# Three chained transformer layers on one core: the squares of queries and keys as a stream of their own, the last weights of an output product in the keys' buffers, a zero-padded compressed-value product

## The chip, the cores and the metric

One core of one Trainium2 chip runs the whole program. The core has five engines with an instruction queue each: PE (the 128x128 matrix array), DVE (elementwise work and reductions), ACT (activation functions and copies), POOL (general work) and SP (which here issues DMA transfers). Each engine runs its own queue in order, and an instruction waits there until its semaphores are reached. The metric is the device time of one execution in microseconds (us), median of several runs.

## The reference

512 tokens of width 1024 pass three layers. Only what the change touches is written out:

```
layer 1   q, kc_raw, vc_raw, ks, vs, kw, vw, gates, hq, hf, hi, hg = split(rms_norm(x) @ w_in)
          q  = rms_norm(q per head of 64)             # 8 heads; needs the sum of squares of each row of a head
          ks, kw = rms_norm(...)                      # 2 key groups each, the same sums
          kc, vc = rms_norm(compress(kc_raw)), compress(vc_raw)      # 31 compressed keys and values
          o_nsa  = g0 * softmax(q kc) vc + g1 * softmax(q ks) vs + g2 * softmax(q kw) vw
          o_hgrn = gated linear recurrence over chunks of 64 (4 heads)
          x = x + concat(o_nsa, o_hgrn) @ w_out       # 1024 x 1024
          x = x + (silu(gate) * up) @ w_down          # gated feed-forward, width 2816
layers 2, 3   stick-breaking attention (8 heads of 64) and differential attention (4 heads),
          x = x + concat(sb, df) @ w_o                # 1024 x 1024
          x = x + relu(h @ w_ff1)^2 @ w_ff2           # width 4096
```

All is float32.

## The kernel before

The residual stream X lies in SBUF as eight tiles [128 features x 512 tokens]. A product by a weight matrix streams the weights in blocks of 512 KB through `load_w` (L376): SP issues the DMA into one of three raw buffers, ACT casts it to a rounded copy `hi` (L395), DVE writes the remainder `lo` (L396), both into rings of two buffers. Each product tile is then three matmuls, `mm3` (L401 to L403): hi by high half, lo by high half, hi by low half. `gemm_fm` (L411) walks the blocks of a matrix and hands each finished bank of PSUM to an `emit` function; a block of an output product covers four groups k of 128 input rows and two tiles of 128 output features.

The program is written by Python generators that a planner interleaves. `Clock` (L74) keeps an estimate of when each engine is free and when each tile is written and last used; `_drive` (L171) asks the streams in a fixed order for their next step, and a stream whose tiles aren't ready by the estimate (`ready`, `bank_free`) is passed over. In layer 1 the streams are the linear recurrence (`hgrn_all`), the preparation of the sparse attention (`nsa_setup`), its attention proper (`nsa_attention`), and last the dense products (`dense1`), which fill what the others leave. A scheduler then orders each engine's instructions by that priority and their dependencies; weight loads have their priority raised by a lookahead.

What the change touches:

- `emit_nsa` (L776) gets the projections of queries (m = 0 to 3) and keys (m = 4, 5), 64 features of two heads each. It evacuates them (`nq`, `nraw`), has ACT square them (`nsq`, L789), and at once issues four PE matmuls by a block matrix of ones (`pq`, L792; each is two instructions in the trace) and the copy of the sums to `qss` (L795, L798). The dense stream's next matmuls stand behind these on PE. `nsa_setup` goes on from `qss` to the norms.
- `gemm_late` (L464) is the half of the output product whose operand, the last mixer outputs, comes late: for its blocks 0 and 1 it does row groups 0 to 2, then waits for row group 3 (`hs[3]`), finishes the four tiles, and passes blocks 2 and 3 to `gemm_fm`, named `wout0x` in layer 1, `L0wo1x` and `L1wo1x` in layers 2 and 3. It starts when the attention's last scores are issued (`"scored"`): block 0 then takes two spare banks that the scores used (`wl0`, `wl1`; in layers 2 and 3 a pair, `L0wl`), block 1 the two `mm` banks. The weights of block 2 and 3 wait for a free pair of the hi and lo ring.
- `values` (L1021) of the sparse attention runs once for each unit (4 head pairs i, 4 query blocks, 2 branches). In branch 0 it first opens the bank `po` with the compressed values: `comp["v"]` holds four copies of 32 rows, and the product contracts 32 rows of it, placed at row 32 i of the array (L1028).
- In layers 2 and 3 the differential attention runs units of one query block: `scores2`, `turn2` (transposes, `dpt`), `values2` (`dfo`, L1337), and `head_squares` (L529), where ACT squares the output of the unit out of the same bank `dfo` that the next unit's matmuls write to. After a head's last unit its norm is taken, the output is transposed (`do_t`, L558) and split into `do_m_h` (ACT, L561) and `do_m_l` (DVE, L562), which are `hs` of `gemm_late`.

## Time and profile before

| | us |
|---|---|
| time, median of 3 runs | 2017.0 (2017.0 to 2017.1) |
| profiled execution: its own time | 2017.01 |
| its span in the trace | 2015.1 |
| PE busy | 1974.8 (98%) |
| DVE busy | 1176.9 (58%) |
| ACT busy | 885.1 (44%) |
| POOL busy | 45.2 (2%) |
| mean granted clock of TensorE | 0.993 |

PE is busy for all but some 40 us of the span. The profile gives the granted TensorE clock by stretches: 1.00 stands for 2.4 GHz and 0.50 for 1.2 GHz. PE's waits are listed by the instruction that waited and the one that released it; a window gives the busy time of each engine in a stretch of the span.

### The profile page before, as it was taken

The page shows a single profiled execution, that of the slowest core. Times are in us where ns is not written, and L with a number is a line of the kernel's source. Part 1 is how long each engine was busy: PE and PEld are TensorE (multiplying, and loading weights), DVE is VectorE, ACT ScalarE, POOL GpSimd, SP SyncE. Part 2 cuts the span into 40 slices and gives each one's busy share as a digit, 9 for nine tenths or more (in the row PEclk, how much of TensorE's full clock was granted, in tenths as well). Part 3 has the DMA queues.
Part 4 walks back from the last instruction along what each step waited for, and adds up shares of the span by engine and source line. Part 5 has one row for each costly group of instructions (what it writes and reads, how often), then busy time and mean ns, then how long its engine had stood idle before and what let it go on. Part 6 is the DMA issues. An engine that isn't in the chain of part 4 may idle for free.

```text
span 2015.1 us, 25957 instructions
## 1 busy us (share of the span) xinstructions
PE 1974.8 (98%) x10197; PEld 1610.1 (80%) x10197; DVE 1176.9 (58%) x2032; ACT 885.1 (44%) x1497; POOL 45.2 (2%) x87
## 2 busy tenths in 40 slices
PE   8999999999999999999999999999999999999998
PEld 7888866788888878787778888888888778888887
DVE  7687676744444456557764444447466874444446
ACT  6645355522222235687542223335587743322223
POOL 1000000000000000001000000000000000000000
PEclk9999899999999999999999999999999999999999
DMA  6212100122222222212122222223221222222222
GB/s 206 67 60 88 51 22 22 53 95 96 99 97 95 95 89 92 82 40 84 61 84 98 100 95 94 94 94 105 79 64 58 63 76 98 98 94 94 95 94 74
DMA packets 50922, 168.65 MB, mean 84 GB/s; under 512 B 5808, under 2 KB 8240, under 8 KB 50800
## 3 DMA queue, kind: packets, MB, share of 16 engines
q1 hardware_dynamic: 47680, 161.93, 23.4%
q0 software_dynamic: 2976, 4.98, 1.2%
q8 instruction: 81, 1.33, 0.3%
q14 instruction: 41, 0.34, 0.1%
q10 hardware_dynamic: 144, 0.07, 0.0%
HBM read 160.14 MB, written 2.10 MB: 81 GB/s over the span
## 4 chain that ended last, share of the span: by engine, by line
PE 88%; DVE 5%; ACT 5%; issue 2%; DMA 1%; SPq 0%; DVEq 0%; POOL 0%; ACTq 0%
PE L0wf_p L403 6%; PE L0wf_p L401 6%; PE L0wf_p L402 6%; PE L1wf_p L403 5%; PE L1wf_p L401 5%; PE L1wf_p L402 5%; PE wgu_p L403 4%; PE wgu_p L401 4%; PE wgu_p L402 4%; PE wdn_p L401 2%; PE wdn_p L402 2%; PE wdn_p L403 2%; PE po L1033 1%; PE hpl L695 1%; PE pt L1014 1%
## 5 line engine op out<-in xcount | busy, mean ns | idle before, releaser
L395 ACT CAST L0wf_h<-L0wf_r 128x1024 fp32r<-128x1024 f32 x64 | 67.3, 1051 | 228.1 <-PE L0wf_p L403 224.8
L395 ACT CAST L1wf_h<-L1wf_r 128x1024 fp32r<-128x1024 f32 x60 | 63.1, 1051 | 219.7 <-PE L1wf_p L403 216.7
L403 PE MATMUL wgu_p<-h_l,wgu_h 128*128 128x512 f32 x328 | 128.8, 393 | 0.0
L401 PE MATMUL wgu_p<-h_h,wgu_h 128*128 128x512 f32 x328 | 128.7, 392 | 0.0
L402 PE MATMUL wgu_p<-h_h,wgu_l 128*128 128x512 f32 x328 | 128.6, 392 | 0.0
L395 ACT CAST wgu_h<-wgu_r 128x1024 fp32r<-128x1024 f32 x44 | 46.2, 1050 | 162.9 <-issue 62.8
L401 PE MATMUL L0wf_p<-L0u_h,L0wf_h 128*128 128x512 f32 x256 | 100.7, 393 | 0.0
L402 PE MATMUL L0wf_p<-L0u_h,L0wf_l 128*128 128x512 f32 x256 | 100.4, 392 | 0.0
L403 PE MATMUL L0wf_p<-L0u_l,L0wf_h 128*128 128x512 f32 x256 | 99.4, 393 | 0.0
L403 PE MATMUL L0wf_p<-L0m_l,L0wf_h 128*128 128x512 f32 x240 | 94.2, 393 | 0.0
L403 PE MATMUL L1wf_p<-L1m_l,L1wf_h 128*128 128x512 f32 x240 | 94.2, 393 | 0.0
L401 PE MATMUL L0wf_p<-L0m_h,L0wf_h 128*128 128x512 f32 x240 | 94.2, 392 | 0.0
L401 PE MATMUL L1wf_p<-L1m_h,L1wf_h 128*128 128x512 f32 x240 | 94.2, 392 | 0.0
L402 PE MATMUL L1wf_p<-L1m_h,L1wf_l 128*128 128x512 f32 x240 | 94.1, 392 | 0.0
L402 PE MATMUL L0wf_p<-L0m_h,L0wf_l 128*128 128x512 f32 x240 | 94.1, 392 | 0.0
L396 DVE TENSOR_TENSOR L0wf_l<-L0wf_r,L0wf_h 128x1024 fp32r<-128x1024 f32 x64 | 78.4, 1226 | 24.7 <-ACT L0wf_h L395 24.7
L401 PE MATMUL L1wf_p<-L1u_h,L1wf_h 128*128 128x512 f32 x224 | 88.1, 393 | 0.0
L402 PE MATMUL L1wf_p<-L1u_h,L1wf_l 128*128 128x512 f32 x224 | 87.9, 392 | 0.0
L396 DVE TENSOR_TENSOR L1wf_l<-L1wf_r,L1wf_h 128x1024 fp32r<-128x1024 f32 x60 | 73.5, 1225 | 23.2 <-ACT L1wf_h L395 23.2
L403 PE MATMUL L1wf_p<-L1u_l,L1wf_h 128*128 128x512 f32 x224 | 86.9, 393 | 0.0
L491 DVE TENSOR_TENSOR X<-X,L0wf_p 128x512 f32<-128x512 f32 x64 | 44.0, 687 | 67.1 <-PE L0wf_p L403 67.1
L491 DVE TENSOR_TENSOR X<-X,L1wf_p 128x512 f32<-128x512 f32 x56 | 38.6, 689 | 66.5 <-PE L1wf_p L403 66.5
(879 smaller groups left out, 5397.2 us busy)
## 6 DMA issues: line engine op xcount, KB each, us to landing
L0wf_r<-w_ff SPq DMA_DIRECT2D x64, 512.0 KB, 3.2
L1wf_r<-w_ff SPq DMA_DIRECT2D x60, 512.0 KB, 3.3
wgu_r<-w_gu SPq DMA_DIRECT2D x44, 512.0 KB, 3.2
wdn_r<-w_dn SPq DMA_DIRECT2D x22, 512.0 KB, 3.2
wns_r<-w_nsa SPq DMA_DIRECT2D x8, 512.0 KB, 3.5
L0wsb_r<-w_sbqk SPq DMA_DIRECT2D x8, 512.0 KB, 3.2
L0wdf_r<-w_dfqk SPq DMA_DIRECT2D x8, 512.0 KB, 3.2
L1wsb_r<-w_sbqk SPq DMA_DIRECT2D x8, 512.0 KB, 3.2
```

Of the source, the lines that this page charges most:

```text
L395: S.copy(hi[:, c], raw[:, c])
L396: V.tensor_tensor(lo[:, c], raw[:, c], _f(hi)[:, c], ALU.subtract)
L401: TE.matmul(ps, lh, rh, start=start, stop=False)
L402: TE.matmul(ps, ll, rh, start=False, stop=False)
L403: TE.matmul(ps, lh, rl, start=False, stop=stop)
L491: V.tensor_tensor(X[m], X[m], ps, ALU.add)
L695: TE.matmul(pl[:, b * 64 : (b + 1) * 64], ke[:, b * P : (b + 1) * P], qr[:, b * 64 : (b + 1) * 64], start=True, stop=True)
L1014: TE.transpose(pt[:, o + j * P : o + (j + 1) * P], p[g][:, j * P : (j + 1) * P], ident)
L1033: TE.matmul(po[g * 64 : (g + 1) * 64, 0:P], vsw[:, j, br * 128 + g * 64 : br * 128 + (g + 1) * 64], p[g][:, j * P : (j + 1) * P], start=Fa ...
```

## The change

Four parts.

1. The sums of squares. `emit_nsa` only squares and puts the tile in a list `waiting`. A new stream `nsa_squares`, the first that the planner asks, issues the `pq` matmuls and the copy to `qss` when the square is ready by the estimate and a bank of kind `t` is free; the next `emit_hgrn`, `emit_gate` or `emit_nsa` issues what still waits (`catch_up`).
2. `gemm_late` loads blocks 0 and 1 without waiting for the last scores. Block 0 takes the `mm` banks, block 1 waits for `scored` and takes the spare banks, and at that point the weights of block 2 are loaded into buffers of the keys (`kh`, `kl`), so that `gemm_fm` finds them there.
3. The compressed values lie in `vz`, 128 rows by four blocks of 128 columns, zero but for 32 rows each, written by POOL (a memset and four copies); the product contracts all 128 rows.
4. In layers 2 and 3 the planner holds `values2` of a head's later units until the last reader of the head's bank is done by the estimate (`Clock.read`).

```diff
@@ Clock
+    def read(self, tile):
+        self.take()
+        e, at = self.used.get(tile.tensor.name, ("PE", 0.0))
+        while e != "PE" and self.free["PE"] < at + 0.2:
+            yield None
@@ gemm_fm
-            wh, wl = load_w(src[b], f"{name}_{b}")
+            wh, wl = loaded.pop(0) if loaded else load_w(src[b], f"{name}_{b}")
@@ gemm_late
-    def gemm_late(src, hs, emit, name, banks):
-        tiles, banks = [], list(banks)
+    def gemm_late(src, hs, emit, name, scored, spare_banks):
+        tiles = []
         cols = src.shape[3]
         yield from until(lambda: all(x is not None for x in hs[:3]))
+        loaded = [load_w(src[b], f"{name}_{b}") for b in range(2)]
         for b in range(2):
-            wh, wl = load_w(src[b], f"{name}_{b}")
+            wh, wl = loaded[b]
+            if b == 1:
+                yield from until(scored)
+                loaded = [load_w(src[2], f"{name}_2", ("kh", "kl"))]
+                banks = spare_banks()
             for m in range(cols // P):
-                ps = banks.pop(0)() if banks else bank("mm", f"{name}_p{b}_{m}")
+                ps = bank("mm", f"{name}_p{b}_{m}") if b == 0 else banks[m]
...
-        yield from gemm_fm(src[2:], hs, emit, name + "x", 2 * (cols // P))
+        yield from gemm_fm(src[2:], hs, emit, name + "x", 2 * (cols // P), loaded=loaded)
@@ block1
+        def add_squares():
+            m, sq = waiting.pop(0)
+            pq = bank("t", f"pq{m}")
+            for tb in range(NB):
+                TE.matmul(pq[:, 2 * tb : 2 * tb + 2], sq[:, tb * P : (tb + 1) * P], blk2, start=True, stop=True)
...
+        def catch_up():
+            while waiting:
+                add_squares()
+        def nsa_squares():
+            while len(squared) < 6:
+                yield from until(lambda: waiting or len(squared) == 6)
+                if not waiting:
+                    return
+                m, sq = waiting[0]
+                for w in (ready(sq), bank_free("t", 2)):
+                    for _ in w:
+                        if not waiting or waiting[0][0] != m:
+                            break
+                        yield None
+                if waiting and waiting[0][0] == m:
+                    add_squares()
+                    yield "low"
         def emit_nsa(m, ps):
+            catch_up()
...
             S.activation(sq, ps, AF.Square)
-            pq = bank("t", f"pq{m}")
...
+            waiting.append((m, sq))
@@ nsa_setup
-            yield from until(lambda: 1 in kraw, lambda: nq[3] is not None)
+            yield from until(lambda: len(squared) == 6)
@@ nsa_attention
-                        TE.matmul(po[g * 64 : (g + 1) * 64, 0:P], comp["v"][32 * i : 32 * i + 32, g * 64 : (g + 1) * 64],
-                                  pct[g][32 * i : 32 * i + 32, qs], start=True, stop=False, tile_position=(32 * i, g * 64))
+                        TE.matmul(po[g * 64 : (g + 1) * 64, 0:P], vz[:, i * P + g * 64 : i * P + (g + 1) * 64],
+                                  pct[g][:, qs], start=True, stop=False)
...
+            vz = sb("hs", "vz")
+            G.memset(vz, 0.0)
+            for i in range(4):
+                r = slice(32 * i, 32 * i + 32)
+                G.tensor_copy(vz[r, i * P : (i + 1) * P], comp["v"][r])
@@ dense1
-            yield from until(lambda: "scored" in comp)
...
-        _drive(clock, hgrn_all(), nsa_setup(), nsa_attention(), dense1())
+        _drive(clock, nsa_squares(), hgrn_all(), nsa_setup(), nsa_attention(), dense1())
@@ layer
-                     lambda n: both(ready(st[n], dv[NB - 1]), bank_free("o", 1) if n % NB == 0 else ()))))
+                     lambda n: both(ready(st[n], dv[NB - 1]), bank_free("o", 1) if n % NB == 0 else clock.read(st["do"])))))
```

In the instruction orders below a row is a line of the program, an operation, the tile it writes and those it reads; the line numbers of the changed kernel are seven higher at L401 and up to 51 higher further down. PE around the last of the six sums of squares in layer 1, before (`wvsw` is the product for the values, `hpl` and `qr`, `ke` belong to the linear recurrence):

```order
L403 MATMUL wvsw_p_1982<-wvsw_l,h_6_h 128x280
L401 MATMUL wvsw_p_1982<-wvsw_h,h_7_h 128x280
L402 MATMUL wvsw_p_1982<-wvsw_h,h_7_l 128x280
L403 MATMUL wvsw_p_1982<-wvsw_l,h_7_h 128x280
L792 MATMUL pq_1951<-packed,nsq_1949 128x2 [waits PE_49,Activation_49]
L695 MATMUL hpl_4_1932<-qr_4_1913,ke_4_1914 128x64 [waits DVE_49,PE_49]
L695 MATMUL hpl_4_1932<-qr_4_1913,ke_4_1914 128x64 x3
L792 MATMUL pq_1951<-packed,nsq_1949 128x2 x3
L401 MATMUL wvsw_p_2037<-wvsw_h,h_0_h 128x280
```

And in the changed kernel:

```order
L409 MATMUL wvsw_p_1937<-wvsw_h,h_7_l 128x280
L410 MATMUL wvsw_p_1937<-wvsw_l,h_7_h 128x280
L710 MATMUL hpl_16_1919<-qr_16_1899,ke_16_1900 128x64 [waits DVE_49,Activation_49]
L710 MATMUL hpl_16_1919<-qr_16_1899,ke_16_1900 128x64 x3
L408 MATMUL wvsw_p_2001<-wvsw_h,h_0_h 128x280 [waits DVE_49]
L409 MATMUL wvsw_p_2001<-wvsw_h,h_0_l 128x280
L410 MATMUL wvsw_p_2001<-wvsw_l,h_0_h 128x280
L798 MATMUL pq_1950<-packed,nsq_1917 128x2 [waits Activation_49]
L798 MATMUL pq_1950<-packed,nsq_1917 128x2 x3
L408 MATMUL wvsw_p_2001<-wvsw_h,h_1_h 128x280
```

The eight `pq` instructions stood right behind the last matmul of the first `wvsw` tile, six of them behind four `hpl`; they now stand behind four `hpl` rows and the first three matmuls of the second `wvsw` tile.

ACT at the same place, before (the tile `nsq_1879` belongs to the fifth and `nsq_1949` to the sixth of the sums):

```order
L395 CAST wvsw_h<-wvsw_r 128x1120 [waits DMAHW7_49,PE_49]
L435 CAST nq_1944<-wns_p_0_1906 64x512
L789 ACTIVATE nsq_1879<-wns_p_0_1812 128x512 [waits DVE_49]
L685 ACTIVATE ke_4_1914<-ke_4_1914 128x512 [waits DVE_49]
L686 ACTIVATE ke_4_1914<-ke_4_1914 128x512 [waits Activation_49]
L435 CAST nq_1944<-wns_p_0_1906 64x512 [waits DVE_49]
L801 ACTIVATE vsw<-wvsw_p_1982,st_rn 128x256 [waits PE_49]
L685 ACTIVATE ke_2_1958<-ke_2_1958 128x512 [waits DVE_49]
L686 ACTIVATE ke_2_1958<-ke_2_1958 128x512 [waits Activation_49]
L789 ACTIVATE nsq_1949<-wns_p_0_1906 128x512 [waits DVE_49]
L678 ACTIVATE qr_1_1995<-qr_1_1995 128x256 [waits DVE_49]
```

And in the changed kernel, where these are `nsq_1824` and `nsq_1917`:

```order
L402 CAST wvsw_h<-wvsw_r 128x1120 [waits DMAHW7_49,PE_49]
L840 ACTIVATE nsq_1824<-wns_p_0_1725 128x512 [waits DVE_49]
L737 COPY at_1830<-hpo_1826 128x512 [waits PE_49]
L741 COPY at_1834<-hpo_1832 128x256 [waits PE_49]
L442 CAST nq_1912<-wns_p_0_1850 64x512
L442 CAST nq_1912<-wns_p_0_1850 64x512 [waits DVE_49]
L844 ACTIVATE vsw<-wvsw_p_1937,st_rn 128x256 [waits PE_49]
L840 ACTIVATE nsq_1917<-wns_p_0_1850 128x512 [waits DVE_49]
L700 ACTIVATE ke_4_2035<-ke_4_2035 128x512 [waits DVE_49]
L701 ACTIVATE ke_4_2035<-ke_4_2035 128x512 [waits Activation_49]
```

The fifth square has moved ahead of the next query's cast but still stands behind the cast of `wvsw_h`; the sixth has moved ahead of two `ke` activations and still stands behind the evacuation of the first `wvsw` tile, whose order against the others is unchanged.

PE at the end of layer 2's differential attention, from the transposes of the last head on, before:

```order
L558 MATMUL L0do_t<-packed,L0do_8609 128x128 [waits DVE_49,PE_49]
L558 MATMUL L0do_t<-packed,L0do_8609 128x128 x3
L402 MATMUL L0wo_p_0_8638<-L0do_m_h,L0wo_1_l 128x512
L403 MATMUL L0wo_p_0_8638<-L0do_m_l,L0wo_1_h 128x512
L401 MATMUL L0wo_p_0_8638<-L0do_m_h,L0wo_1_h 128x512
L402 MATMUL L0wo_p_0_8638<-L0do_m_h,L0wo_1_l 128x512
L403 MATMUL L0wo_p_0_8638<-L0do_m_l,L0wo_1_h 128x512
L401 MATMUL L0wo_p_1_8648<-L0do_m_h,L0wo_1_h 128x512
L402 MATMUL L0wo_p_1_8648<-L0do_m_h,L0wo_1_l 128x512
L403 MATMUL L0wo_p_1_8648<-L0do_m_l,L0wo_1_h 128x512
L401 MATMUL L0wo_p_1_8648<-L0do_m_h,L0wo_1_h 128x512
L402 MATMUL L0wo_p_1_8648<-L0do_m_h,L0wo_1_l 128x512
```

In the changed kernel:

```order
L571 MATMUL L0do_t<-packed,L0do_8628 128x128 [waits DVE_49,PE_49]
L571 MATMUL L0do_t<-packed,L0do_8628 128x128 x3
L409 MATMUL L0wl<-L0do_m_h,L0wo_1_l 128x512
L410 MATMUL L0wl<-L0do_m_l,L0wo_1_h 128x512
L408 MATMUL L0wo_p_0_8585<-L0do_m_h,L0wo_0_h 128x512 [waits Activation_49]
L409 MATMUL L0wo_p_0_8585<-L0do_m_h,L0wo_0_l 128x512
L408 MATMUL L0wo_p_1_8606<-L0do_m_h,L0wo_0_h 128x512
L409 MATMUL L0wo_p_1_8606<-L0do_m_h,L0wo_0_l 128x512
L410 MATMUL L0wo_p_0_8585<-L0do_m_l,L0wo_0_h 128x512 [waits DVE_49]
L410 MATMUL L0wo_p_1_8606<-L0do_m_l,L0wo_0_h 128x512
L408 MATMUL L0wl<-L0do_m_h,L0wo_1_h 128x512
L409 MATMUL L0wl<-L0do_m_h,L0wo_1_l 128x512
```

Before, 14 more matmuls that don't need row group 3 stand between these transposes and the first that needs it; now there are two, and block 2's matmuls (`L0wo1x`, from `L0wo_2kh`) begin two rows behind the piece.

## Rows read from the trace of the kernel before

**Rows 1.** The page, part 1: busy time of each engine and its share of the span.

```profile
PE 1974.8 (98%) x10197; PEld 1610.1 (80%) x10197; DVE 1176.9 (58%) x2032; ACT 885.1 (44%) x1497; POOL 45.2 (2%) x87
```

**Rows 2.** PE's waits over the span: us in total, times, longest.

```profile
PE pq L792 <- ACT nsq L789: 4.5, 4, 2.2
...
PE L0wo_p L401 <- DVE X L491: 1.3, 1, 1.3
...
PE L0dfo L1337 <- ACT L0dsq L532: 1.2, 2, 0.9
...
PE L0wo1x_p L401 <- ACT L0wo1x_h L395: 0.8, 1, 0.8
...
PE L0wo1x_p L402 <- DVE L0wo1x_l L396: 0.6, 1, 0.6
...
PE wout0x_p L402 <- DVE wout0x_l L396: 0.6, 1, 0.6
```

**Rows 3.** Windows: length, PE, PEld, DVE, ACT, POOL busy; then granted clock, DMA.

```profile
200.76:204.18 3.42, 3.42 (x17) 3.42 (x16) 2.56 (x4) 1.85 (x3) 0.00 (x0) 0.50 0.33 126
...
207.59:221.24 13.65, 13.18 (x59) 13.19 (x60) 5.83 (x21) 1.18 (x3) 0.00 (x0) 0.50 0.01 2
...
1013.13:1016.55 3.42, 3.42 (x9) 2.65 (x8) 2.76 (x4) 2.34 (x5) 0.00 (x0) 0.50 0.75 220
```

**Rows 4.** Timeline, PE, 196 to 210 us: start, duration, instructions, idle before.

```profile
196.68 1.00 PE L695 MATMUL hpl<-qr,ke 128*128 128x64 f32 x8
199.15 1.05 PE L792 MATMUL pq<-packed,nsq 128*128 128x2 f32 x8 [1.47 <-ACT nsq L789]
...
205.41 0.29 PE L402 MATMUL wvsw_p<-wvsw_h,h_l 128*128 128x280 f32 x1
205.54 0.29 PE L403 MATMUL wvsw_p<-wvsw_l,h_h 128*128 128x280 f32 x1
208.06 0.59 PE L792 MATMUL pq<-packed,nsq 128*128 128x2 f32 x2 [2.23 <-ACT nsq L789]
208.50 1.95 PE L695 MATMUL hpl<-qr,ke 128*128 128x64 f32 x8
```

**Rows 5.** Timeline, ACT, 196 to 208 us.

```profile
196.88 1.13 ACT L395 CAST wvsw_h<-wvsw_r 128x1120 fp32r<-128x1120 f32 x1 [3.54 <-PE wns_p L403]
...
198.51 0.59 ACT L789 ACTIVATE nsq<-wns_p 128x512 f32<-128x512 f32 x1
...
205.86 0.47 ACT L801 ACTIVATE vsw<-wvsw_p,st_rn 128x256 f32<-128x256 f32 x1 [2.58 <-PE wvsw_p L403]
...
207.42 0.58 ACT L789 ACTIVATE nsq<-wns_p 128x512 f32<-128x512 f32 x1
```

**Rows 6.** Timeline, PE, 191 to 192 us.

```profile
191.01 0.59 PE L719 MATMUL hpo<-qx,kx 128*128 128x256 f32 x2
...
191.91 0.58 PE L402 MATMUL wns_p<-h_h,wns_l 128*128 128x512 f32 x1
```

**Rows 7.** Windows in layer 1's sparse attention, columns as in rows 3.

```profile
252.00:256.00 4.00, 2.13 (x17) 1.87 (x17) 3.79 (x23) 3.14 (x10) 0.00 (x0) 1.00 0.00 0
347.76:360.65 12.89, 11.37 (x80) 6.97 (x80) 9.43 (x32) 7.29 (x20) 0.00 (x0) 1.00 0.00 1
```

**Rows 8.** Timeline, PE, end of layer 2's attention.

```profile
1003.63 0.63 PE L558 MATMUL L0do_t<-packed,L0do 128*128 128x128 f32 x4 [0.17 <-DVE L0do L551]
1004.02 0.48 PE L402 MATMUL L0wo_p<-L0do_m_h,L0wo_l 128*128 128x512 f32 x1
```

**Rows 9.** Timeline, ACT, at the same place.

```profile
1004.30 0.69 ACT L561 ACTIVATE L0do_m_h<-L0do_t,L0sg 128x512 fp32r<-128x512 f32 x1 [2.32 <-PE L0do_t L558]
```

**Rows 10.** Timeline, PE, 363 to 366 us.

```profile
363.13 0.43 PE L1028 MATMUL po<-cpt,vcn 32*64 32x128 f32 x4
363.50 0.43 PE L1033 MATMUL po<-p,vsw 128*64 128x128 f32 x2
...
364.52 1.09 PE L1033 MATMUL po<-p,vsw 128*64 128x128 f32 x14
```

More of the change, by code (lines that the diff above doesn't have):

```diff
@@ L774, in block1 @@
         comp = {}
+        waiting, squared = [], []
+        def add_squares():
[3 more added lines that the diff above has]
+                TE.matmul(pq[:, 2 * tb : 2 * tb + 2], sq[:, tb * P : (tb + 1) * P], blk2, start=True, stop=True)
+            if m < 4:
+                V.tensor_copy(qss[:, 0:32].rearrange("p (b i g) -> p b i g", b=NB, i=4)[:, :, m, :],
+                              pq[:, 0:8].rearrange("p (b g) -> p b g", g=2))
+            else:
+                V.tensor_copy(qss[:, 32 + 8 * (m - 4) : 40 + 8 * (m - 4)], pq[:, 0:8])
+            squared.append(m)
+        def catch_up():
[15 more added lines that the diff above has]
+                    yield "low"
         def emit_nsa(m, ps):
+            catch_up()
             if m >= 4:
@@ L789, in emit_nsa @@
             S.activation(sq, ps, AF.Square)
-            pq = bank("t", f"pq{m}")
-            for tb in range(NB):
-                TE.matmul(pq[:, 2 * tb : 2 * tb + 2], sq[:, tb * P : (tb + 1) * P], blk2, start=True, stop=True)
-            if m < 4:
-                V.tensor_copy(qss[:, 0:32].rearrange("p (b i g) -> p b i g", b=NB, i=4)[:, :, m, :],
-                              pq[:, 0:8].rearrange("p (b g) -> p b g", g=2))
-            else:
-                V.tensor_copy(qss[:, 32 + 8 * (m - 4) : 40 + 8 * (m - 4)], pq[:, 0:8])
+            waiting.append((m, sq))
         def emit_vsw(tb, ps):
@@ L1043, in values @@
                 return 0.25 * (b + 1)
[L1046 removed]
+            yield from until(lambda: len(nk) == 2, lambda: "gates" in comp, lambda: "linear" in comp, lambda: "v" in comp)
+            vz = sb("hs", "vz")
[3 more added lines that the diff above has]
+                G.tensor_copy(vz[r, i * P : (i + 1) * P], comp["v"][r])
             yield from pipeline(len(units), 2, (
@@ L1095, in dense1 @@
                     yield from gemm_fm(d["w_out"][n], mix[4 * n : 4 * n + 4], add_residual, f"wout{n}")
-            yield from until(lambda: "scored" in comp)
-            yield from gemm_late(d["w_out"][0], Late(mix, 0), add_residual, "wout0",
-                                 [lambda: bank("s", "wl0"), lambda: bank("s", "wl1")])
+            yield from gemm_late(d["w_out"][0], Late(mix, 0), add_residual, "wout0", lambda: "scored" in comp,
+                                 lambda: [bank("s", f"wl{i}") for i in range(2)])
         run(gemm_fm(d["w_hqf"][0:2], h1, emit_hgrn, "whqf0", 0, spare(2, "sph")))
-        _drive(clock, hgrn_all(), nsa_setup(), nsa_attention(), dense1())
+        _drive(clock, nsa_squares(), hgrn_all(), nsa_setup(), nsa_attention(), dense1())
         h2 = normed(C["norm_ffn"], "h2_")
@@ L1403, in dense, with last_banks @@
                     yield from gemm_fm(d["w_o2"][l, 0, n : n + 1], mixed[0:4], add_residual, f"{L}wo{n}", 2 * n)
-            yield from until(lambda: "scored" in st)
-            last = two_banks(L + "wl")
-            yield from gemm_late(d["w_o2"][l, 1], Late(mixed, 4), add_residual, L + "wo1", [lambda: last[:, 0], lambda: last[:, 1]])
+            def last_banks():
+                t = two_banks(L + "wl")
+                return [t[:, 0], t[:, 1]]
+            yield from gemm_late(d["w_o2"][l, 1], Late(mixed, 4), add_residual, L + "wo1", lambda: "scored" in st, last_banks)
         _drive(clock, attention(), dense())
```

6 lines of the change are left out of this document (3 added, 3 removed).

## The prediction

> **What bounds the kernel now.** I read the page's shares first, then PE's waits, then the granted clock by windows, and only then single instructions. PE is busy for 1974.8 us, 98% of the span; DVE follows at 58% [rows 1]. So no other engine can set the pace over long stretches, and the change removes no matmul worth naming: it can win only from the 40 us in which PE stands (2015.1 less 1974.8) and from busy time that is long because the clock is low. The reader should see in the list of waits that no wait is large: the largest, PE's `pq` for the squares, is 4.5 us in four waits [rows 2]. The windows show what the list hides: behind two of these waits the granted clock is 0.50, that is 1.2 GHz instead of 2.4, for 3.42 and 13.65 us, and it is 0.50 again for 3.42 us behind the wait for `L0wo1x` [rows 3]. A group of eight `hpl` takes 1.00 us at full clock and 1.95 us there [rows 4]. At half clock, half of PE's busy time is lost: 3.42/2 = 1.7 us, 13.18/2 = 6.6 us and 1.7 us, 10.0 us together.
>
> The sum is made against the profiled execution (2017.01 us, a span of 2015.1 and 1.9 around it), which is the median of 2017.0 to a hundredth.
>
> **The sums of squares.** The fifth `pq` starts at 199.15 after 1.47 us of idleness, the sixth at 208.06 after 2.23 [rows 4]; the other two waits share what is left of 4.5, 0.8 us [rows 2]. Why they are long stands in ACT's rows: the fifth square ends at 199.10, behind a cast of `wvsw_h` that could begin only when the previous product's last matmul was done (196.88, 1.13 us) and a query cast; the sixth stands behind the evacuation of the first `wvsw` tile (205.86) and two `ke` activations, and ends at 208.00 [rows 5].
>
> After the change the fifth square is right behind that cast: 1.13 + 0.59 = 1.7 us after the last matmul of the product. In front of its `pq` PE now has three `hpo` rows; their like took from 191.01 to 191.91, 0.9 us [rows 6]. About 0.9 us of waiting is left with the semaphores. The sixth square needs the evacuation and itself, 0.47 + 0.58 = 1.05 us from the tile's last matmul [rows 5], against eight `hpl` (1.0 us) and three `wvsw` matmuls (0.13 each by their starts [rows 4], 0.4 together): covered, 0.2 us left at most. The two small waits have more matmuls in front and go. New waits 1.1, so 3.4 us gained; bounds 2.0 (the sixth hidden only half) and 4.5. What is late next is the `wvsw_l` half that the first `wvsw` matmul needs, behind the same cast; `pq` and the `pvc` matmuls now stand in front of it, so I count nothing. The squares' copy to `qss` on DVE and the norms behind it come no later than before.
>
> **The clock behind them.** Not shown by any row is what a 0.9 us wait followed by thin work (the `pq` matmuls have two columns) does to it. Bounds: all 8.3 us of 1.7 + 6.6 come back, or none. I take that the first, short fall stays, since 1.47 us brought it about and 0.9 is nearer to that than to nothing, and that the second goes with the 2.23 us wait: 6.6 us gained. For the whole to go speaks the window 252 to 256 us, where PE stood for 1.87 of 4.00 us at a granted clock of 1.00 [rows 7].
>
> **The output products.** The wait for block 2's cast and remainder is 0.8 + 0.6 in layer 2 and the same rows again in layer 3, 0.6 in layer 1 [rows 2]: 3.4 us. Block 2 now waits in the keys' buffers when PE comes to it, and block 3's cast has block 2's 24 matmuls for cover. With the layer 2 wait goes the half clock at 1013, 1.7 us. But something is given back. Block 0 is now used up during the attention, and at its end only two matmuls stand between the last transposes and the first matmul that needs `do_m_h`, where there were fourteen. From the start of the transposes (1003.63 [rows 8]) to the end of `do_m_h` (1004.30 + 0.69 [rows 9]) it is 1.36 us; PE needs 0.4 for the transposes (the next start is 1004.02 [rows 8]) and 0.5 for the two matmuls, which hold 512 columns as that one does. So 0.5 us of new waiting in each of layers 2 and 3, 1.0. In layer 1 six matmuls stand there and the chain is a copy of one bank: nothing. `do_m_l` is late by one more DVE operation, and four more matmuls cover it. Net 3.4 + 1.7 - 1.0 = 4.1 us; bounds 5.1 and 2.0 (the new wait twice as long, and the earlier cast, about the 1.13 us of `wvsw_h`, in front of a unit's exponential in one layer). The wait for `X`, 1.3 us in each of layers 2 and 3 [rows 2], sits in the matmuls that are displaced; it may go or grow, 2.6 us either way, and I count zero.
>
> **The head's bank.** The `dfo` matmuls waited 1.2 us in two waits of each layer for the square that reads their bank [rows 2]. The longest, 0.9 us, gets one more 512-column matmul in front, 0.2 us; the other, 0.3 us, should go. About 0.4 per layer, 0.8; bounds 0 and 2.4.
>
> **Compressed values over 128 rows.** Four instructions of 32 rows take 0.37 us to the next start (363.13 to 363.50); fourteen of 128 rows take 1.09 to the end of the last, 0.08 each, so four of these 0.31 [rows 10]. There are 16 such groups: at most 16 x 0.06 = 1.0 us, at least nothing; half, 0.5. POOL, busy for 2%, fills `vz` long before; the five instructions delay nothing I can find.
>
> **Layer 1's attention.** The moved fillers are its price. The order has one piece of 92 PE instructions there without a dense matmul, where the longest before has about half. The nearest stretch of before, 80 instructions from 347.76 to 360.65, has PE idle for 12.89 - 11.37 = 1.5 us [rows 7], so some 1.7 for 92; a little comes back elsewhere, as other units have more fillers. I put it at 1.5 us lost, bounds 1.5 gained and 4 lost.
>
> Sum: 3.4 + 6.6 + 4.1 + 0.8 + 0.5 - 1.5 = 13.9 us, so 2017.0 - 13.9 = 2003.1 us.
>
> **Rivals.**
> (A) The long fall stays. The new order still has idleness of 0.9 us and, behind it, `pq`, `hpl` and `wvsw` in the same mixture in which the clock stayed at 0.50 for 13.65 us though PE was busy for 13.18 of them [rows 3]; against it, the wait that went before it is gone. The waits go, 6.6 us don't: 2009.7.
> (B) Slower. The long piece without fillers in layer 1's attention lets the clock fall, and it stays down to the attention's end, which is the 12.89 us of rows 7 and about as much behind them, 26 us of work. Then 26 us are added to the sum: 2029. It is slower by over 4 us once 18 us of that work run at half clock. The long fall shows that busy time need not end one; the windows of rows 7, with 1.87 of 4.00 and 1.5 of 12.89 us idle at full clock, speak against.
> The Trainium skill, "TensorE: Matmul & The Clock Gate", "A second HAM failure mode: psum-queue depth-cycling", says that short idle times between groups of matmuls are enough to make the clock go back and forth, and that the loss lies between the bursts. By that rule (B) would come about, since the waits of the attention are of this kind; the trace of before, with the same kind of waits and 1.00 throughout rows 7, doesn't bear it out so far.
> (C) Only the products pay. The squares come earlier, but the preparation of the attention behind them is a chain of DVE and ACT steps; if PE then lacks work at the attention's start for as long as it has saved, the waits reappear there and with them a fall of the clock. Then 4.1 + 0.8 + 0.5 - 1.5 = 3.9 us remain: 2013.1. For it speaks that 252 to 256 us is already thin [rows 7]; against it, that the dense stream still has blocks left there.
>
> **Chances.** Forecast 0.60, (A) 0.20, (C) 0.14, (B) 0.06. A change of 0.2%, 4.0 us, is about what a measurement of this kernel can tell from none. Faster by more: 0.59 of the forecast, 0.19 of (A), 0.06 of (C), 0.84. Slower by more: 0.05 of (B). Within: the rest, 0.11. The range for 8 in 10: below, the forecast with the first fall gone too (1.7), the waits at their best (1.1 and 1.0) and the attention's loss nothing (1.5) is 2003.1 - 5.3 = 1997.8; above, it takes in (A) and part of (C). 1997.5 to 2012.5 us.
>
> **What the next profile would show.** Right: `pq` waits of about 1 us in all; the granted clock 1.00 from 205 to 221 us; no wait for `L0wo1x` or `wout0x`, a full clock at the end of layer 2's attention, and there a new wait of about 0.5 us of PE for `do_m_h`; a `dfo` wait of 0.6 us left. Wrong: a fall that lasts over 10 us behind the sums (A), any fall between 330 and 375 us (B), or new waits of the first scores and `cpt` of over 3 us (C). The forecast is off by more than its terms if the waits for `X` change by over 1 us in both layers.

## The result and the profile after

The changed kernel takes 1998.67 us (median of four runs, 1997.79 to 1998.99); the kernel before, measured beside it, 2017.0 (2009.91 to 2017.1). The ratio is 0.9919, with an interval of 0.9900 to 0.9938. The forecast was 2003.1, so the change gained 18.3 us where 13.9 were expected. One thing has to be known for all that follows: the kernel before is not one number. In its runs beside the experiments it lay between 2008.8 and 2018.7 us, with medians of 2014.5 to 2015.4, and the mean granted clock on record goes with the time: 0.991 in the run of 2018.7 us, 0.996 in that of 2008.8. Against those medians the change is worth some 16 us.

The changed kernel's profiled execution took 1998.82 us with a span of 1997.0. The page's busy times, to be read against [rows 1]:

```profile
PE 1964.2 (98%) x10197; PEld 1602.2 (80%) x10197; DVE 1173.9 (59%) x2032; ACT 885.3 (44%) x1497; POOL 48.5 (2%) x92
```

PE has as many instructions as before, but is busy for 10.6 us less and idle for 32.8 us (1997.0 less 1964.2) where it was 40.3. So more than half of the gain is not a wait that went, but work that took less time, most of it because it ran at a higher clock. PE's waits over the span, in the changed kernel (us in total, times, longest), which answer to [rows 2]:

```profile
PE ho_t L571 <- DVE ho L564: 4.2, 2, 3.9
...
PE s L1024 <- ACT p L1036: 1.7, 4, 0.9
...
PE pq L798 <- ACT nsq L840: 1.1, 2, 0.8
...
PE L0dfo L1385 <- ACT L0dsq L545: 0.6, 1, 0.6
...
PE L0wo_p L408 <- ACT L0do_m_h L574: 0.3, 1, 0.3
```

The squares' wait fell from 4.5 to 1.1 us. The waits for `L0wo1x` and `wout0x`, and that of `L0wo_p` for `X`, have no row any more. The first row is new: 3.9 us of one wait for the last output of the linear recurrence. The windows of the changed kernel, with columns as in [rows 3], show the clock at four places: behind the sums, at the attention's start, later in the attention, and at the end of layer 2's attention:

```profile
195.00:225.00 30.00, 30.00 (x247) 28.68 (x247) 22.99 (x60) 10.55 (x18) 5.83 (x11) 1.00 0.24 67
240.75:247.57 6.82, 4.22 (x16) 3.47 (x17) 5.94 (x20) 2.45 (x7) 0.00 (x0) 0.50 0.00 0
330.00:375.00 45.00, 43.43 (x293) 32.01 (x290) 32.38 (x86) 24.37 (x59) 0.00 (x0) 1.00 0.11 36
985.00:1022.00 37.00, 36.49 (x177) 29.01 (x176) 26.45 (x52) 18.66 (x38) 1.62 (x3) 1.00 0.23 76
```

Both falls behind the sums are gone, and so is the one at 1013 us. One new fall, of 6.82 us, stands around the new wait; half of the 4.22 us that PE was busy in it, 2.1 us, is lost to it. Before, the falls cost 10.0 us. (Both traces also end at half clock, for 8.7 and 8.6 us in which PE is busy for 0.8 and 0.7.)

To see where the 18.2 us of span (2015.1 less 1997.0, to a tenth) came from, I compared the start of the first instruction of each stage in the two traces:

| first instruction of | before | after | gained so far |
|---|---|---|---|
| layer 1's first projection | 7.35 | 6.71 | 0.6 |
| layer 1's feed-forward | 405.44 | 394.35 | 11.1 |
| layer 2 | 768.88 | 758.74 | 10.1 |
| layer 2's feed-forward | 1037.59 | 1022.25 | 15.3 |
| layer 3 | 1392.91 | 1377.60 | 15.3 |
| layer 3's feed-forward | 1658.49 | 1639.57 | 18.9 |
| end | 2015.14 | 1996.96 | 18.2 |

The gain at the start is not the change's. PE's first 650 instructions are the same in both kernels, and yet the two traces differ there. Two of the first projection's matmuls, before and then after:

```profile
8.38 0.63 PE L401 MATMUL sph<-h_h,whqf_h 128*128 128x512 f32 x1
8.80 0.63 PE L402 MATMUL sph<-h_h,whqf_l 128*128 128x512 f32 x1
```

```profile
7.28 0.39 PE L408 MATMUL sph<-h_h,whqf_h 128*128 128x512 f32 x1
7.51 0.40 PE L409 MATMUL sph<-h_h,whqf_l 128*128 128x512 f32 x1
```

Before, they start 0.42 us apart, as the others do up to 13.06 us; after, 0.23 us apart at the same place. The windows print 1.00 for this stretch in both traces, so this reading rests on the durations alone. The lead of 0.6 us has become 1.4 when PE reaches its 200th instruction (44.25 us before, 42.85 after) and is the same at the 600th. So 0.8 us of what the table books to layer 1's mixer belongs to the start of these two executions.

The mixers of layers 1, 2 and 3 gained 10.5, 5.2 and 3.6 us. By the prediction's terms they should have gained 9.6 (3.4 + 6.6 + 0.6 + 0.5 - 1.5), 3.0 (1.4 + 1.7 - 0.5 + 0.4) and 1.3 (the same without the clock). So the largest shares of the excess lie in layers 2 and 3.

### The profile page after: what moved, and what is told of

Its sections match the earlier page's. It is cut to its first block, busy times and chain, and to the rows that moved or that the text cites. A ratio compares the mean times of both kernels' runs of the same rounds, so it can differ in the third digit from the quotient of the medians.

```text
span 1997.0 us, 25958 instructions
## 1 busy us (share of the span) xinstructions
PE 1964.2 (98%) x10197; PEld 1602.2 (80%) x10197; DVE 1173.9 (59%) x2032; ACT 885.3 (44%) x1497; POOL 48.5 (2%) x92
## 4 chain that ended last, share of the span: by engine, by line
PE 89%; ACT 5%; DVE 4%; issue 2%; DMA 1%; SPq 0%; POOL 0%; DVEq 0%; ACTq 0%
PE L0wf_p L410 6%; PE L0wf_p L408 6%; PE L0wf_p L409 6%; PE L1wf_p L408 5%; PE L1wf_p L410 5%; PE L1wf_p L409 5%; PE wgu_p L408 4%; PE wgu_p L410 4%; PE wgu_p L409 4%; PE wdn_p L408 2%; PE wdn_p L410 2%; PE wdn_p L409 2%; PE hpl L710 1%; PE po L1076 1%; PE pt L1057 1%
```

## The experiments

Each kernel starts either from the changed one (`a_`) or from that of before (`b_`). The first four take one part of the change out, four put one part (or a substitute) alone into the kernel before, and four try to mend the new wait. Each ran beside the kernel before, and the ratios are to that one; where an `a_` kernel is set against the changed one, medians of different rounds are compared, between which the median of the kernel before moved by 0.9 us. Their traces are of one execution each.

### The squares issued at once

```diff
             waiting.append((m, sq))
+            catch_up()
```

> The changed kernel, but the sums of squares are issued at once again, right behind the square. Theory T (the change's parts each remove the waits that the profile of before names, and with the squares goes the low clock behind them): the pq waits (4.5 us instead of 1.1) and the two falls of the clock between 195 and 225 us (1.7 + 6.6 us) come back, +11.7 us, 2010.4; less if the new ho_t wait of 3.9 us at the attention's start and its fall (2.1 us) go at the same time, then 2004.4. Rival R (the late product's new order makes the time, the squares little): within 2 us of 1998.7.

2006.41 us (2001.0 to 2007.59, six runs), ratio 0.9957 (0.9941 to 0.9972). The trace is 7.6 us longer than that of the changed kernel, all of it before layer 1's feed-forward; 1.1 us of it is there after 600 instructions that both kernels share, so 6.5 are the squares'. The wait is back and with it both falls; its windows:

```profile
200.67:204.09 3.42, 3.42 (x17) 3.42 (x16) 2.31 (x4) 1.84 (x3) 0.00 (x0) 0.50 0.28 108
207.50:221.15 13.65, 13.41 (x60) 13.41 (x61) 5.68 (x22) 1.08 (x3) 0.00 (x0) 0.50 0.01 2
```

and the row `PE pq L798 <- ACT nsq L840: 4.5, 4, 2.2`. The 3.9 us wait for `ho` is not there, nor the fall around it. So the squares' stream gives waits and clock back, and brings the new wait with it, and some 6.5 us are left of 3.4 + 8.3. The time lies between the two that theory T names.

### The output products as before

```diff
-(gemm_late and its calls of the changed kernel)
+(those of the kernel before)
```

> The changed kernel with the late half of the output product as before (block 0 waits for the last scores, block 2 for the ring). Theory T: the waits for block 2 come back (1.4 us in each of layers 2 and 3, 0.6 in layer 1), the half clock at the end of layer 2 (1.7 us), and the waits for X (1.3 us in each of layers 2 and 3), less the 0.3 us waits for do_m_h: 3.4 + 1.7 + 2.6 - 0.6 = 7.1, 2005.8. Rival R2 (the waits for X went because of the wait for the head's bank, not of the late product): without them 4.5, 2003.2.

2002.24 us (2001.98 to 2002.86, five runs), ratio 0.9940 (0.9926 to 0.9955). Its waits:

```profile
PE L0wo1x_p L408 <- ACT L0wo1x_h L402: 0.7, 1, 0.7
...
PE wout0x_p L409 <- DVE wout0x_l L403: 0.6, 1, 0.6
...
PE L0wo1x_p L409 <- DVE L0wo1x_l L403: 0.5, 1, 0.5
...
PE L0wl L408 <- ACT L0do_m_h L568: 0.3, 1, 0.3
```

The weights' waits are back, in layer 3 too, but the wait of 1.3 us for `X` is not, and the clock at the end of layer 2's attention stays at 1.00. The late product is worth 3.3 us in the trace, 3.6 by the medians, and has nothing to do with `X`. Nor with the new wait for `do_m_h`, which is still here: this kernel too has only two matmuls between the last transposes and the first that needs `do_m_h`.

### Without the wait for the head's bank

```diff
-bank_free("o", 1) if n % NB == 0 else clock.read(st["do"])
+bank_free("o", 1) if n % NB == 0 else ()
```

> The changed kernel without the planner's wait for the last reader of the head's bank in layers 2 and 3. Theory T: the waits of dfo for the square are 1.2 + 0.4 us per layer again instead of 1.0: +1.1 us, 1999.8. Rival R2: with the waits for X (2.6 us) as well, 2002.4. Rival 0 (the planner's wait only moves the waits): 1998.7.

2003.71 us (2003.29 to 2005.01, five runs), ratio 0.9948 (0.9932 to 0.9965). Its waits:

```profile
PE L1wo_p L408 <- DVE X L504: 1.3, 1, 1.3
PE L0wo_p L408 <- DVE X L504: 1.3, 1, 1.3
...
PE L0dfo L1385 <- ACT L0dsq L545: 1.1, 2, 0.8
```

With the last experiment this settles where the waits for `X` went: one line of the planner took them away. The wait of layer 2 in the trace of before:

```profile
974.82 0.50 PE L401 MATMUL L0wo_p<-L0mix_h,L0wo_h 128*128 128x512 f32 x1 [1.29 <-DVE X L491]
```

It stands in the first half of the output product (`L0mix_h`), 29 us ahead of the last head's transposes, and not among the late matmuls. That the units of a head, held back until its bank has been read, stand otherwise against the dense stream there, so that the addition to `X` is done when its reader comes, is the likely reason; the runs show only that the line removes the wait. The same line brings the wait for `do_m_h`: it has no row here, where fourteen matmuls stand again between the last transposes and the first that needs `do_m_h`, though the late product is that of the changed kernel. Layers 2 and 3 are 1.7 and 1.3 us longer here, 3.0 together.

The other 2 us come from something that I had not looked for. Up to layer 2's attention the two kernels issue the same instructions in the same order. Yet 0.6 us are lost at the kernel's start, and here the clock falls at 195.18 us and there it doesn't, which costs 1.4. First this kernel's windows before and in the fall, then the changed kernel's of the same lengths:

```profile
185.00:195.18 10.18, 9.09 (x67) 7.39 (x65) 8.78 (x19) 5.36 (x10) 0.00 (x0) 1.00 0.25 75
195.18:198.59 3.41, 3.41 (x18) 3.41 (x17) 2.04 (x4) 0.39 (x1) 0.00 (x0) 0.50 0.24 90
```

```profile
185.00:195.18 10.18, 9.09 (x69) 7.48 (x68) 8.31 (x17) 4.79 (x9) 0.00 (x0) 1.00 0.30 100
195.18:198.59 3.41, 3.41 (x27) 3.11 (x25) 3.13 (x7) 0.58 (x1) 0.00 (x0) 1.00 0.05 16
```

PE was busy for 9.09 us in both, with the same wait of 0.75 us before `pq`. So whether the short fall comes is not set by the instructions alone. Whether it is chance from one execution to the next is not shown: the five runs of this kernel lie within 1.7 us and all at least 4.3 above the four of the changed one, at a mean clock of 0.994 to 0.995 against 0.996 to 0.997, which would fit a fall in each of them.

### The compressed product over 32 rows

```diff
-TE.matmul(po[...], vz[:, ...], pct[g][:, qs], start=True, stop=False)
+TE.matmul(po[...], comp["v"][32 * i : 32 * i + 32, ...], pct[g][32 * i : 32 * i + 32, qs], start=True, stop=False, tile_position=(32 * i, g * 64))
```

> The changed kernel with the compressed values' product over 32 rows again. Theory T: 16 groups at 0.03 us each, +0.5 us, 1999.2, bounds 1998.7 and 1999.7. Rival S (the time hangs on the order that the scheduler finds rather than on the product's length): off by more than 2 us, either way, with the difference at the attention's start.

2001.06 us (1999.38 to 2002.12, five runs), ratio 0.9933 (0.9918 to 0.9948). In the trace the attention is 1.3 us longer; the rest of the difference is a short fall at 195.77 us (1.4) and the start (1.0). Two rows of this kernel, then two of the changed one, show the group of four and what follows it:

```profile
255.51 0.43 PE L1071 MATMUL po<-cpt,vcn 32*64 32x128 f32 x4
255.88 0.66 PE L1076 MATMUL po<-p,vsw 128*64 128x128 f32 x8
```

```profile
252.75 0.44 PE L1071 MATMUL po<-cpt,vz 128*64 128x128 f32 x4
253.02 0.61 PE L1076 MATMUL po<-p,vsw 128*64 128x128 f32 x8
```

From the start of one group to the next it is 0.37 us over 32 rows and 0.27 over 128: 0.10 each, times 16 groups 1.6 us, of which 1.3 arrive.

### The kernel before, with PE kept at work

17 matmuls of 512 columns whose result is overwritten, 7 before the fifth and 10 before the sixth sum.

```diff
             pq = bank("t", f"pq{m}")
+            for r in range({2: 7, 3: 10}.get(m, 0)):
+                TE.matmul(pq, h1[0][0][:, 0:P], h1[0][0], start=True, stop=True)
```

> The kernel before with seven and ten extra 512-column matmuls, whose results are overwritten, in front of the fifth and sixth sums' matmuls; they are about as long (3.9 us) as the two waits (1.47 and 2.23 us). Theory T (PE's standing still lets the clock fall, and the fall costs more than the wait): both falls between 195 and 225 us go, 8.3 us less though PE has 3.9 us more to do, about 2009, and the runs lie closer together than those of the kernel before (2009.8 to 2018.7). Rival K (the thin mixture of sums, hpl and wvsw brings the low clock, not the waits): the falls stay, 2015 or more.

2007.97 us (2006.12 to 2010.9, 12 runs) beside 2014.53 for the kernel before (2008.88 to 2018.09, 29 runs): ratio 0.9971 (0.9960 to 0.9981). The windows of this kernel:

```profile
195.00:225.00 30.00, 29.77 (x245) 28.41 (x245) 20.73 (x54) 10.95 (x18) 3.10 (x6) 1.00 0.19 45
```

More work for PE (3.9 us) and a kernel that is some 6.6 us faster. Nothing was moved here, no chain shortened: what the two long waits cost was above all the clock behind them. The same trace has two falls that the profiled execution of before doesn't have, one at 247.95 us in the attention, and this one in layer 3, behind the waits for `L1wo1x`:

```profile
1626.93:1630.34 3.41, 3.41 (x8) 2.73 (x9) 3.07 (x4) 2.64 (x5) 0.00 (x0) 0.50 0.69 205
```

### One part alone in the kernel before

```diff
+(the squares' stream alone: nsa_squares, catch_up, and the setup's wait for six sums)
```

> The kernel before with only the sums of squares as a stream of their own. Theory T: layer 1 as in the changed kernel but for the compressed values, so the 7.6 us that taking this part away cost: about 2007.5 against a kernel before at 2015; the ho_t wait of 3.9 us and the fall behind it are there. Rival R (the part pays only together with the late product, whose fillers it uses up earlier): less than 4 us, 2011 or more.

2009.5 us (2008.21 to 2010.42, 11 runs), ratio 0.9980 (0.9969 to 0.9991): 5.0 us less than 2014.53. The window 195 to 225 has a full clock, the wait for `ho` is there (4.2 us in two waits), and the trace has two falls of 3.41 us in the attention, at 243.41 and 349.22. There is none at 1013, though the waits for the weights stand there as before. So the result lies between the two theories.

```diff
-    bank_free("o", 1) if n % NB == 0 else ()
+    bank_free("o", 1) if n % NB == 0 else clock.read(st["do"])
```

> The kernel before with only the planner's wait for the last reader of the head's bank in layers 2 and 3. Theory R2 (from the run without it): the waits for X (1.3 us per layer) go and the dfo waits shrink, 3.0 us together, about 2012 against a kernel before at 2015; layer 2's low clock at its end stays or goes by the run. Theory T of the prediction: 0.8 us, 2014.

2011.97 us (2004.39 to 2013.15, 12 runs), ratio 0.9990 (0.9978 to 1.0002): by its interval not told from no change. In the trace layer 2's mixer is 3.7 us shorter (1.7 of it the fall at its end, which no other trace has there) and layer 3's 2.2, and layer 2's feed-forward 0.9 longer; the waits for `X` are gone, as in the changed kernel, and the waits for `do_m_h` are there (0.3). In layer 1, where PE's instructions and the waits of 1.47 and 2.23 us are those of before, the falls are longer than before, 20.5 us at half clock:

```profile
197.83:204.66 6.83, 6.83 (x32) 6.83 (x32) 3.57 (x8) 1.85 (x3) 0.00 (x0) 0.50 0.23 78
208.07:221.72 13.65, 13.54 (x61) 13.54 (x62) 5.67 (x23) 0.95 (x3) 0.00 (x0) 0.50 0.01 2
```

```diff
+(gemm_late and its calls of the changed kernel alone)
```

> The kernel before with only the late half of the output product changed. Theory T: the waits for block 2 go (1.4 us in each of layers 2 and 3, 0.6 in layer 1), less new waits of 0.3 for do_m_h, and the half clock at the end of layer 2 goes where it occurs: 3 to 4.5 us less than a kernel before at 2015, 2010.5 to 2012. Rival R (alone it gives fillers away, and the attention's waits grow): 2014 or more.

2006.59 us (2002.64 to 2010.84, seven runs), ratio 0.9962 (0.9947 to 0.9978). More than the late product should be worth. The runs lie 8 us apart, and the profiled execution is the fastest of them (2002.64); its trace says why. The squares' waits are those of [rows 2], 4.5 us, with the two long ones of [rows 4] to the hundredth; but behind them this execution has only a short fall:

```profile
200.00:207.76 7.76, 5.53 (x46) 5.30 (x45) 6.47 (x14) 4.37 (x8) 0.00 (x0) 1.00 0.10 40
207.76:211.17 3.41, 3.41 (x18) 3.41 (x17) 1.13 (x6) 0.00 (x0) 0.00 (x0) 0.50 0.01 2
211.17:225.00 13.83, 13.83 (x132) 13.52 (x131) 8.38 (x26) 4.30 (x7) 3.11 (x6) 1.00 0.27 58
```

The same waits (PE idle for 2.23 of the first 7.76 us), with PE's instructions in the same order up to 318 us, brought 17.1 us at half clock in the profiled execution of before [rows 3], 20.5 in the experiment before this one and 3.4 here. The waits for `X` are still 1.3 us in each layer, and there is none for `do_m_h`, which agrees with the experiments above. Layers 2 and 3 are 4.0 and 2.3 us shorter in their mixers, 4.6 together without the fall at 1013; the feed-forwards of layers 1 and 3 are 0.7 and 0.6 longer.

### Attempts on the new wait

The wait for `ho` looks like a matter of DVE's order. DVE in the changed kernel, 236 to 243 us (start, duration, instruction, idle before):

```profile
236.62 0.17 DVE L554 TENSOR_SCALAR ho_v<-hss 128x4 f32<-128x4 f32 x1 [0.58 <-ACT hsq L545]
...
238.07 1.21 DVE L985 TENSOR_REDUCE cs<-sc 128x32 f32<-128x1024 f32 x1
...
240.54 1.22 DVE L991 TENSOR_TENSOR sc<-sc,cs 128x1024 f32<-128x1024 f32 x1
...
242.62 0.68 DVE L564 TENSOR_TENSOR ho<-hpv,ho_rn 128x512 f32<-128x512 f32 x1
```

and PE, which waits for the last of these:

```profile
239.24 0.23 PE L1026 MATMUL s<-masks 128*128 128x128 bf16 x1
243.35 1.11 PE L571 MATMUL ho_t<-packed,ho 128*128 128x128 f32 x4 [3.88 <-DVE ho L564]
```

Six microseconds from `ho_v` to `ho`, a chain of small operations of 0.15 us each, with the compressed scores' long ones and the first units' softmax between them. PE's transposes stand at the head of its queue meanwhile, with the attention's matmuls behind them.

```diff
                     if b > 0:
-                        yield "low"
+                        yield True
                     for i in range(4):
                         TE.matmul(pc[:, b, i, :], ...)       # the compressed scores
```

> The changed kernel, in which the matmuls for the scores of the compressed keys don't give way to the dense stream, so that they end some 30 instructions of PE earlier and DVE's four long operations on these scores lie ahead of the attention's first units. Theory D (the new 3.9 us wait at the attention's start is DVE's queue: the last recurrent head's norm stands between these operations and the first units' softmax): the ho_t wait falls under 1.5 us and the fall of the clock behind it goes, 3.0 + 2.1 us, 1993.5. Rival P (another chain, the head's own squares or PE's order, sets it): 1998 to 1999.

1999.48 us (1996.15 to 2000.77, six runs), ratio 0.9932 (0.9917 to 0.9947): no gain. The wait for `ho` is down to 0.8 us, but the scores' is 3.0, and the clock falls three times. That much speaks for DVE's order; the time didn't follow. The compressed scores' matmuls now follow each other, PE doesn't stand still in them, and yet the clock goes to half behind the row of 24 and at the end of the row of 32. This kernel's PE, and its windows at and behind the two rows:

```profile
207.51 2.76 PE L970 MATMUL cs<-kcT,nq 128*128 128x32 f32 x24
...
221.10 3.87 PE L970 MATMUL cs<-kcT,nq 128*128 128x32 f32 x32
```

```profile
207.33:210.74 3.41, 3.41 (x33) 3.41 (x31) 1.60 (x7) 0.42 (x1) 0.00 (x0) 1.00 0.02 5
210.74:214.15 3.41, 3.41 (x18) 3.15 (x16) 1.57 (x8) 0.00 (x0) 0.00 (x0) 0.50 0.00 0
220.97:224.39 3.42, 3.42 (x34) 3.42 (x32) 2.01 (x6) 0.00 (x0) 1.62 (x4) 1.00 0.61 196
224.39:227.80 3.41, 3.41 (x14) 3.17 (x14) 0.64 (x3) 1.23 (x2) 0.00 (x0) 0.50 0.16 59
```

Two of the four long operations on POOL:

```diff
-            V.tensor_tensor(sc32, sc32, rqc32[:, :, None]..., ALU.mult)
+            G.tensor_tensor(sc32, sc32, rqc32[:, :, None]..., ALU.mult)
-            V.tensor_tensor(sc32, sc32, cs[:, :, None]..., ALU.mult)
+            G.tensor_tensor(sc32, sc32, cs[:, :, None]..., ALU.mult)
```

> The changed kernel with two of the four long operations on the compressed scores (the scaling by the norms and the last scaling by the gates, 1.2 us of DVE each) on POOL. Theory D (the ho_t wait at the attention's start is DVE's queue): that queue is 2.4 us shorter, the wait of 3.9 us falls to about 1.5 us and the fall of the clock behind it may go: 1994.5 to 1996.5. Rival Q (the compressed scores' own chain is the bound, and it gets longer where POOL takes longer than DVE): the wait moves to cpt or to the first po, 1998.7 or more.

2000.5 us (1998.93 to 2001.7, six runs), ratio 0.9933 (0.9914 to 0.9951): no gain, and the wait for `ho` is still 3.8 us: rival Q has the time, but not the place of the wait. POOL and DVE of this kernel at the second operation:

```profile
240.24 1.91 POOL L991 TENSOR_TENSOR sc<-sc,cs 128x1024 f32<-128x1024 f32 x1 [3.43 <-DVE cs L990]
```

```profile
240.65 1.52 DVE L311 TENSOR_TENSOR nr_a<-nr_a,ho_rn 128x4 f32<-128x4 f32 x1
242.09 0.15 DVE L1039 TENSOR_TENSOR sm<-sm,gl 128x2 f32<-128x2 f32 x1
```

The small operation of the chain, 0.15 us elsewhere, took 1.52 and ended when POOL did (240.24 + 1.91 = 242.15): the work moved, the wait stayed.

The compressed scores ahead of the norms:

```diff
+            yield from until(lambda: nq[3] is not None)
+            (the loop of the compressed scores' matmuls, moved here)
             yield from until(lambda: len(squared) == 6)
```

> The changed kernel in which the matmuls for the compressed scores come ahead of the norms in the preparation, still giving way to the dense stream, so that no more than 16 of these thin matmuls stand in a row. Theory D with the clock: the ho_t wait falls under 1.5 us as in the run before this one, without that run's two falls behind rows of 24 and 32 thin matmuls: 1994 to 1996. Rival P (the attention's first units only start later, and what they wait for moves with them): 1998 to 2001.

2006.48 us (2003.49 to 2008.65, eight runs), ratio 0.9961 (0.9946 to 0.9976). Both theories missed: the loop still gives way to every other stream, and now the norms stand behind it. The first scores start at 245.78 instead of 229.16 us, and the wait for `ho` is still 3.6 us.

15 filler matmuls ahead of those transposes:

```diff
         pt = bank("t", name + "_t")
+        for r in range(15 if name == "ho3" else 0):
+            TE.matmul(pt, keep[0][:, 0:P], keep[0], start=True, stop=True)
```

> The changed kernel with fifteen extra 512-column matmuls (3.5 us, results overwritten) ahead of the last recurrent head's transposes; they come first, and the late rows of the output product then fill what they leave. Theory C (the new wait at the attention's start costs its length and, by the fall of the clock, more): PE works 3.5 us more and waits about as much less, and the fall of 6.8 us at half clock goes, 2.1 us: 1996 to 1997. Rival N (the units behind it are DVE's, so that the wait only moves behind the extra matmuls): 1999 to 2002.

2000.38 us (1999.13 to 2003.55, six runs), ratio 0.9931 (0.9919 to 0.9944). The clock is 1.00 from 225 to 255 us and the wait for `ho` 0.3, and still layer 1's attention is 0.5 us longer than in the changed kernel: 3.5 us of fillers against 3.6 of waiting and 2.1 of clock should have left it 2.2 shorter. Where the other 2.7 went I did not trace; the order behind the fillers is another one. Another 0.8 is lost in layer 2, where PE now waits 1.1 us for `L0do`. None of the four beats the changed kernel.

## Why the prediction was right

The range (1997.5 to 2012.5) holds the time, close to its lower end. By its steps:

- **Squares' waits, 3.4 us.** Measured 4.5 - 1.1 = 3.4. The fifth `pq` waits 0.75 us (0.9 was worked out); the sixth, and the small waits, leave 0.3.
- **The clock behind them, 6.6 us.** In the profiled execution 8.3: the first fall went too. It was taken to stay since 0.9 us is nearer to 1.47 than to nothing; it does come in other executions behind the same wait, at 195.18 and 195.77 us. So the size of this term differs from trace to trace for the same instructions, and that it came so near is in part luck: the 17.1 us of before [rows 3] are 20.5 in one other trace and 3.4 in another. Rival (A) did not come about: the clock is 1.00 from 195 to 225 us, and the four runs lie within 1.2 us.
- **The output products, 4.1 us.** Waits of 3.4 gone, 1.7 of clock back, the new wait for `do_m_h` 0.3 where 0.5 was worked out, in each of layers 2 and 3. Taken out alone they cost 3.3 us in the trace. Two steps of this term were wrong. The 1.7 can't be counted in full: five traces have the waits for `wo1x` in layers 2 and 3, ten places, and the clock falls behind two of them (layer 2 before, layer 3 with the fillers); the nine traces without these waits have no fall there. So the waits may bring a fall, but seldom, and so few cases don't settle it. And the wait for `do_m_h` is no price of the early blocks: the two matmuls in place of fourteen, and the wait, come with `read` (also in the kernels with the late product of before) and not with the late product alone. What the late product does give back was not foreseen: in the traces that have it the feed-forwards of layers 1 and 3 are longer, by 0.9 and 1.0 us against the changed kernel without it, 0.7 and 0.6 alone in the kernel before.
- **The head's bank, 0.8 us: mis-sized.** Its own `dfo` wait fell from 1.2 to 0.6 as named, but the part is worth 3.0 us, since it also takes away the 1.3 us for `X` in each of layers 2 and 3. The prediction put these among the matmuls that the late product displaces, which is wrong (they stand in the first half of the output product), counted zero, and named them as what would make the forecast off by more than its terms. They did. What it missed is that `read` changes the order of PE's other matmuls too, of which the bank's wait is only the part that the waits' row shows.
- **Compressed values, 0.5 us: mis-sized.** 1.3 us. The estimate took half of 0.06 us for each group; it is 0.10 in the rows above, though the group itself lasts as long in either shape (0.43 and 0.44 us): what differs is when the next one starts.
- **Layer 1's attention, -1.5 us: right sign, wrong place and size.** The loss was looked for in the long piece without fillers. The window 330 to 375 us shows 1.57 us of idleness at a full clock there, no more than before. Nor is that piece about twice the longest of before: in the traces the longest without a dense matmul has 79 instructions before and 124 after, with PE idle for 1.5 and 0.5 us in them. The loss is at the start: PE arrives earlier than a chain of DVE does. That is close to rival (C), but the chain is the last recurrent head's norm and not the preparation of the attention, and (C)'s sign, waits of the first scores and `cpt` of over 3 us, is not there. PE's waits from the sums to layer 1's feed-forward, before (215 to 405 us) and after (205 to 394 us):

```profile
PE s L981 <- ACT p L993: 2.2, 2, 1.6
PE pt L1014 <- DVE p L998: 1.2, 2, 0.6
PE cpt L957 <- DVE sc L948: 0.8, 1, 0.8
```

```profile
PE ho_t L571 <- DVE ho L564: 3.9, 1, 3.9
PE s L1024 <- ACT p L1036: 1.7, 4, 0.9
PE pt L1057 <- ACT p L538: 0.6, 1, 0.6
```

  With the smaller rows 5.3 us before (0.6 of it for `wout0x`) and 6.9 after, and 2.1 of clock: 4.3 us lost besides the 0.6 gained, just beyond the bound of 4. (C) fell short since this is well under the 11.7 us that waits and clock returned.
- **Rival (B)** did not come: 6.82 us at half clock, around one wait of 3.88 us, and none after it until the kernel's last 8.6 us.

Layer 1's rows give 1.4 (start) + 3.4 + 8.3 + 1.3 - 1.6 - 2.1 = 10.7 us of the 11.1 that the table shows at its feed-forward; the other 0.4 I did not trace. The 1.0 that is given back by layer 2's start goes with the late product, as said. Taken out one at a time, and without what the traces lose in the first 600 instructions, the four parts cost 6.5, 3.2, 3.0 and 1.3 us, 14.0 together; with the 1.7 of the fall at 1013 and the 1.4 at the start that is 17.1 of 18.2.

So the waits that the forecast names went as it says, and the clock with them, but the total lies in the range partly by luck, since errors of both signs meet in it: the first fall (1.7 us), the start (1.4), the output products (1.0), the bank (2.2) and the compressed values (0.8) gave more than was counted, the attention (2.2) and the feed-forwards (1.7) took more. That is 3.2 of the 4.4 us by which the forecast was exceeded.

## What to carry to other kernels

A wait of 1 or 2 us on PE, as those of the squares here, is to be priced with the clock behind it, and that price is a range, not a number: run the kernel several times before a fall in one trace is booked as the cost of a wait. Compare the instructions ahead of the first difference too: what two traces differ by there is not the change. When dense work is pulled ahead or a chain is shortened, look at which chain of the other engines PE now meets first, and count the operations between its links in the order of that engine. A condition that holds one step of a planner back moves everything behind it, so its worth is read from the stage's end and not from the wait for which it was made.

## What was not expected of the hardware

- Identical instructions with the same waits met different clocks: 17.1, 20.5 or 3.4 us at 0.50 behind the sums before, 3.4 or none after. No row of these traces tells what decides. The Trainium skill, "TensorE: Matmul & The Clock Gate", "What's actually happening", says that the moment at which the clock changes at a kernel's start differs from run to run, since the monitor behind it doesn't begin with the kernel. The traces agree for the start (matmuls 0.42 us apart up to 13.06 us before, 0.23 at the same place after). They show such differences in the middle of a kernel too; that these have the same cause no run here shows.
- The clock fell behind 24 and at the end of 32 matmuls of 32 columns (2.76 and 3.87 us) though PE was busy throughout the 3.41 us before. The Trainium skill, "TensorE: Matmul & The Clock Gate", "A second HAM failure mode: psum-queue depth-cycling", speaks of idle times between groups of matmuls; here there was none.
- A DVE operation on 128x4 elements took 1.52 us instead of 0.15 while POOL worked on a tile in SBUF. The Trainium skill, "SBUF — State Buffer", "SBUF: two separate sides", says that the two engines share a port pair which only one of them can hold at a time; the trace agrees, as the operation ended within 0.02 us of POOL's.
